# Low weight parts by adding DMA transfers, transposes on row halves, and a new pace of the convolution taps in a two-layer trunk

## The chip, the core and the metric

The kernel runs on one NeuronCore of a Trainium2 chip. The metric is the device time of one execution in microseconds (us). Engines are called as in the profile: PE (TensorE matmul) and PEld (its weight loads), DVE (VectorE), ACT (ScalarE), POOL (GpSimd) and SP (SyncE, which issues most DMAs). Each engine works its own instructions strictly in order and waits on semaphores for the others.

## What is computed

Two layers over 256 latent tokens and, in the first layer, 256 context tokens, model width 1024, all in float32. One layer is, shortened:

```
h = modulate(rmsnorm(x)); p = h @ w_in            # convolution, q/k/v and gate columns
u = a * sigmoid(g); u = dwconv1d(u, 31 taps); y_conv = silu(layernorm(u)) @ w_conv_out
y_attn = attention(q, k, v: windows + context keys) @ w_na_out      # 8 heads of 64
x = x + g1 * ((sigmoid(gc) * y_conv + sigmoid(ga) * y_attn) @ w_out)
x = x + g2 * conv_ffn(modulate(rmsnorm(x)))
```

The context stream goes through the same weights in the first layer only. The second layer has 256 latent tokens.

## The kernel before, in words

Activations lie with channels on partitions. To keep float32 accuracy at the speed of the rounded type fp32r, each weight and each activation is held as a high part (rounded) and a low part (the rest), and every product is three matmuls: high weight by high activation (L179), high weight by low activation (L180), low weight by high activation (L181). Weights come in units of 128 x 1024, eight 128 x 128 tiles. One unit in the first layer is 24 matmuls of 512 columns.

A unit is made ready by `wparts` and `wunit`: SP loads it into a `raw` buffer, ACT rounds it into `whi` (L160), DVE subtracts (`wlo = raw - whi`, L161). Each of the three names has 4 buffers, so a unit can be prepared while at most three others are still to be used, and ACT's copy waits until PE has finished the unit four back.

The order of the first layer around the change is: eight steps that make V and the first gated convolution input; then q and k of head pair 0 (two units), and for the pairs 1 to 3 two units of gated convolution input (`glu_groups`) and two of q and k; then five of the sixteen branch gates while attention ends; then the other gates, the convolution's layer norm, the branches and the output projection. A generator mechanism puts other work between: `group` calls `slot()` in the middle and at the end of a unit of 512 columns, and each `slot` advances all side jobs by one step. The side job `conv_run` issues `rate` convolution taps on DVE per slot (L591, 4 tiles of 31 taps). The gated inputs `us` are two buffers in the first layer (four in the second), so that `glu(2)` and `glu(3)` first issue every tap of the tile that had the buffer.

The side job `att` does attention in three stages, each a `step` later than the one before: `products` (q by k, matmuls with 64 rows, the two heads of a pair on the two row halves of the array, L440) followed by the softmax on DVE and ACT; `turn` (the softmax weights are transposed, PE into PSUM, ACT copies to `pT`, L494 and L499); `values` (V by the turned weights, L512). A step issues the turn of the last item, the values of the one before, and the products of the next, in that order. The first layer has six items (four latent pairs, two joint context items), the second four. The order in which instructions stand on each engine is fixed by a scheduler when the program is built.

Of the kernel before, what the change touches and what calls it, by code (L numbers as in the profile page):

```python
# [8 lines left out]
F32 = mybir.dt.float32  # L9
# [36 lines left out]
def trunk(ctx: ExitStack, tc: tile.TileContext, xt, cvec, crow, wall, wada, params, bias_t, rope_t, out):  # L46
# [136 lines left out]
    def group(ps, ws, xh, xl, c):  # L183
# [201 lines left out]
    class Attention:  # L385
# [3 lines left out]
        def __init__(self, l, eb, T, V, oh, ol):  # L389
            self.l, self.eb, self.T, self.V, self.oh, self.ol = l, eb, T, V, oh, ol  # L390
            self.todo, self.soft, self.pv, self.n, self.at = [], [], [], 0, 0
            self.ctx, self.pairs, self.last = [], 0, None

# [22 lines left out]
        def step(self, now=False):  # L416
            self.n += 1
            since = self.n - self.at
            if not now and (since < (4 if self.todo else 3 if self.soft else 2) or not self.todo and self.pairs < 4):
                return  # L420
            if self.todo and not now and self.n - self.todo[0][0] < 2:
                return
            self.at = self.n
# [7 lines left out]
            if self.todo:  # L431
                _, what, its = self.todo.pop(0)
                outs = [self.products(it, [psum(t) for t in tags]) for it, tags in zip(its, (("sc", "sc"), ("pt", "main")))]
                self.soft.append((what, its, [(self.scores if what == LAT else self.ctx_scores)(it, o) for it, o in zip(its, outs)]))

# [50 lines left out]
        def turn(self, what, its, pps):  # L486

            pts = [self.eb.tile([P, 4, S], F32, tag="pT", bufs=4, name=nm("pT")) for _ in range(2)]
            for n, tags in enumerate((("sc", "sc"), ("pt", "main"))):
                for i, pp in enumerate(pps[n]):  # L490
                    pt = psum(tags[i])
                    if what == LAT:
                        for kt in range(4):
                            pe.transpose(sl(pt, kt), sl(pp, kt), ident)  # L494
                        act.copy(pts[i][:, :, n * P : (n + 1) * P], pt.rearrange("p (k q) -> p k q", k=4))
                    else:
                        for t in range(2):
                            for kt in range(2):
                                pe.transpose(pt[:, kt * S + t * P : kt * S + (t + 1) * P], sl(pp, 2 * t + kt), ident)  # L499
                        act.copy(pts[i][:, 2 * n : 2 * n + 2, :], pt.rearrange("p (k q) -> p k q", k=2))  # L500
            js = [its[0][0]] if what == LAT else [it[0] for it in its]
            self.pv.append((what, js, pts))

        def values(self, what, js, pts, bank):
            po = psum(bank)
            kts = range(4) if what == LAT else range(2, 4)
            for n, j in enumerate(js):
                c = slice(n * S, (n + 1) * S)
                for kt in kts:
                    for i in range(2):  # L510
                        h = 2 * j + i
                        pe.matmul(  # L512
                            po[i * HD : (i + 1) * HD, c], self.V[kt][:, h * HD : (h + 1) * HD],
                            pts[i][:, 2 * n + kt - kts[0], :], start=kt == kts[0], stop=kt == kts[-1],
                        )
# [42 lines left out]
    for l in range(DEPTH):  # L558
# [5 lines left out]
        with ExitStack() if last else start as e1a:  # L564
# [27 lines left out]

            rate = [0]

            def conv_run():
                while True:
                    for _ in range(rate[0]):
                        if taps:
                            conv_tap(*taps.pop(0))
                    yield  # L600
# [32 lines left out]
            with ExitStack() as e1b:  # L633
# [111 lines left out]
                conv = conv_run()  # L745
                rate[0] = 3 if last else 2
                add_side(conv)
# [477 lines left out]
```

## Time and profile before

| | |
|---|---|
| median of 3 runs | 1127.63 us (1127.43 to 1128.85) |
| the profiled execution | 1127.64 us, its span 1125.9 us |
| granted clock of PE | 0.998 |
| PE busy | 1114.1 us, 99% of the span |
| DVE, ACT, POOL busy | 908.3, 563.6, 14.7 us |
| DMA read | 188.62 MB |

A row of the groups names line, engine, operation, output and inputs, shapes and count, then busy time, the mean of one in ns, and the idle time before them with what ended it. Matmuls overlap, so the distance between the starts of two says more about PE's pace than their durations. A row of the timeline is start and duration in us, engine, line, operation, count, and in square brackets the idle time before it with its releaser. A plain float32 matmul of the program stands as two in the trace; transposes and fp32r matmuls as one.

### The profile page before, as it was taken

The page shows a single profiled execution, that of the slowest core. Times are in us where ns is not written, and L with a number is a line of the kernel's source. Part 1 is how long each engine was busy: PE and PEld are TensorE (multiplying, and loading weights), DVE is VectorE, ACT ScalarE, POOL GpSimd, SP SyncE. Part 2 cuts the span into 40 slices and gives each one's busy share as a digit, 9 for nine tenths or more (in the row PEclk, how much of TensorE's full clock was granted, in tenths as well). Part 3 has the DMA queues.
Part 4 walks back from the last instruction along what each step waited for, and adds up shares of the span by engine and source line. Part 5 has one row for each costly group of instructions (what it writes and reads, how often), then busy time and mean ns, then how long its engine had stood idle before and what let it go on. Part 6 is the DMA issues. An engine that isn't in the chain of part 4 may idle for free.

```text
span 1125.9 us, 17731 instructions
## 1 busy us (share of the span) xinstructions
PE 1114.1 (99%) x6828; PEld 963.0 (86%) x6828; DVE 908.3 (81%) x1631; ACT 563.6 (50%) x934; POOL 14.7 (1%) x24
## 2 busy tenths in 40 slices
PE   9999999999999999999999999999999999999997
PEld 7778777787789988888888888989888999999997
DVE  5689999685778788888898555789996898988773
ACT  4347657542333543434343222544677667766642
POOL 0000000000000000000000000000000000000000
PEclk9999999999999999999999999999999999999999
DMA  9833231536734354554556665556433575565781
GB/s 364 282 94 103 75 118 38 206 97 214 245 118 138 114 161 150 168 169 149 168 171 215 219 191 186 180 181 187 145 126 121 167 250 163 188 194 181 219 268 58
DMA packets 53941, 190.83 MB, mean 169 GB/s; under 512 B 6240, under 2 KB 6496, under 8 KB 53856
## 3 DMA queue, kind: packets, MB, share of 16 engines
q1 hardware_dynamic: 53568, 189.65, 52.1%
q8 instruction: 54, 0.88, 0.3%
q14 instruction: 31, 0.25, 0.1%
q10 hardware_dynamic: 288, 0.04, 0.0%
HBM read 188.62 MB, written 1.05 MB: 168 GB/s over the span
## 4 chain that ended last, share of the span: by engine, by line
PE 83%; DVE 9%; issue 6%; ACT 2%; DMA 0%; POOL 0%; POOLq 0%; DVEq 0%; SPq 0%; ACTq 0%
PE main L179 24%; PE main L181 24%; PE main L180 24%; DVE cb L591 4%; PE main L644 4%; DVE wlo L161 1%; PE sc L181 1%; PE sc L179 1%; PE sc L180 1%; PE po L202 1%; PE po L512 1%; PE sc L129 1%; PE sc L440 0%; DMA sb<-in_crow 0%; PE sc L494 0%
## 5 line engine op out<-in xcount | busy, mean ns | idle before, releaser
L179 PE MATMUL main<-h,whi 128*128 128x256 f32 (+1 forms) x1328 | 446.7, 337 | 0.0
L181 PE MATMUL main<-h,wlo 128*128 128x256 f32 (+1 forms) x1328 | 442.9, 335 | 1.0 <-DVE wlo L161 1.0
L180 PE MATMUL main<-h,whi 128*128 128x256 f32 (+1 forms) x1328 | 442.2, 334 | 0.1
L160 ACT CAST whi<-raw 128x1024 fp32r<-128x1024 f32 (+1 forms) x244 | 252.3, 1039 | 285.5 <-PE main L180 131.5
L161 DVE TENSOR_TENSOR wlo<-raw,whi 128x1024 fp32r<-128x1024 f32 (+1 forms) x244 | 292.9, 1207 | 112.5 <-ACT whi L160 108.0
L179 PEld LDWEIGHTS main<-h,whi 128*128 128x128 f32 x1328 | 249.4, 188 | 32.1 <-issue 3.6
L181 PEld LDWEIGHTS main<-h,wlo 128*128 128x128 f32 x1328 | 249.3, 188 | 29.6 <-DVE wlo L161 1.5
L180 PEld LDWEIGHTS main<-h,whi 128*128 128x128 f32 x1328 | 249.8, 188 | 28.5 <-DVE h L367 0.5
L591 DVE SCALAR_TENSOR_TENSOR cb<-u,par,cb 128x512 f32<-128x512 f32 (+1 forms) x240 | 140.4, 609 | 1.4
L271 DVE CUSTOM_DVE_ANT_0 t<-raw,sb,par 128x1024 bf16<-128x1024 f32 x100 | 126.7, 1277 | 1.0 <-ACT sb L255 0.7
L179 PE MATMUL main<-fh,whi 128*128 128x256 f32 (+1 forms) x386 | 123.0, 319 | 0.0
L180 PE MATMUL main<-fl,whi 128*128 128x256 f32 (+1 forms) x386 | 122.9, 319 | 0.0
L181 PE MATMUL main<-fh,wlo 128*128 128x256 f32 (+1 forms) x386 | 122.9, 318 | 0.0
L180 PEld LDWEIGHTS main<-fl,whi 128*128 128x128 f32 x386 | 72.7, 188 | 5.6
L179 PEld LDWEIGHTS main<-fh,whi 128*128 128x128 f32 x386 | 72.7, 188 | 5.6
L181 PEld LDWEIGHTS main<-fh,wlo 128*128 128x128 f32 x386 | 72.7, 188 | 5.5
L963 ACT ACTIVATE t<-main,par 128x512 f32<-128x512 f32 (+1 forms) x82 | 50.6, 667 | 39.0 <-PE main L181 39.0
L964 DVE SCALAR_TENSOR_TENSOR t<-main,par,t 128x510 f32<-128x510 f32 (+1 forms) x82 | 47.5, 615 | 10.2 <-ACT t L963 9.8
L967 DVE SCALAR_TENSOR_TENSOR t<-main,par,t 128x510 f32<-128x510 f32 (+1 forms) x82 | 46.6, 609 | 0.0
L366 ACT ACTIVATE h<-t,mod 128x256 fp32r<-128x256 f32 x56 | 25.4, 502 | 36.1 <-DVE t L365 36.1
L898 DVE SCALAR_TENSOR_TENSOR x<-main,mod,x 128x256 f32<-128x256 f32 x48 | 22.1, 479 | 23.5 <-PE main L181 23.3
L644 PE MATMUL main<-whi,h 128*128 128x512 f32 x128 | 40.6, 402 | 0.1
(221 smaller groups left out, 1188.2 us busy)
## 6 DMA issues: line engine op xcount, KB each, us to landing
raw<-in_wall SPq DMA_DIRECT2D x239, 512.0 KB, 4.2
raw<-in_wada SPq DMA_DIRECT2D x88, 512.0 KB, 4.3
bias<-in_bias_t SPq DMA_DIRECT2D x8, 640.0 KB, 4.8
row<-in_wada SPq DMA_DIRECT2D x8, 512.0 KB, 4.7
sb<-in_crow SPq DMA_DIRECT2D x5, 512.0 KB, 6.0
x<-in_xt SPq DMA_DIRECT2D x8, 256.0 KB, 4.4
raw<-in_wall SPq DMA_DIRECT2D x8, 256.0 KB, 7.1
out<-t SPq DMA_DIRECT2D x3, 256.0 KB, 2.1
```

The source lines that it names most:

```text
L160: act.copy(hi[:, c], r[:, c])
L161: dve.tensor_tensor(lo[:, c], r[:, c], hi[:, c].bitcast(F32), ALU.subtract)
L179: pe.matmul(ps, w[0], xh, start=start, stop=False)
L180: pe.matmul(ps, w[0], xl, start=False, stop=False)
L181: pe.matmul(ps, w[1], xh, start=False, stop=stop)
L271: dve.tensor_tensor_reduce(tmp().bitcast(BF16), r, v, 1.0, pr(l, BADA + n, 1), ALU.mult, ALU.add, mods[l][:, n, s : s + 1])
L366: high = act.activation(hi[:, c], y[:, c], AF.Identity, bias=b)
L591: dve.scalar_tensor_tensor(cb[j], src, w, cb[j], ALU.mult, ALU.add)
L644: mm = pe.matmul(pv[t], h1[n == 1][k][:, c], w[n == 2][:, b], start=k + n == 0, stop=k == KD - 1 and n == 2)
L963: act.activation(c, pv_, AF.Identity, bias=pr(l, FDB + t, 1), scale=w[1])
L964: dve.scalar_tensor_tensor(c[:, :, 1:], pv_[:, :, : S - 1], w[0], c[:, :, 1:], ALU.mult, ALU.add)
L967: dve.scalar_tensor_tensor(c[:, :, : S - 1], pv_[:, :, 1:], w[2], c[:, :, : S - 1], ALU.mult, ALU.add)
```

## The change

It has four parts and two things that go with them.

1. For the 19 units of the first layer after V and the first gated input (`ADDED`: six of gated input, eight of q and k, five gates) the low part is no longer a DVE subtraction. ACT rounds the unit into `whi` as before, ACT writes `-whi` into `wlo`, and a DMA issued by POOL adds `raw` to it in place.
2. `turn` transposes halves of 64 rows: 32 transposes of 64 columns in the place of 16 of 128, alternating between the two row halves, which go to two PSUM banks. ACT's four copies pick the halves together into one tile `pT`.
3. The first layer has four buffers of gated input, so that no tile has to be finished early, and issues 2.25 taps per slot in place of 2.
4. In each layer the first turn stands alone: its step issues no products, and the next step issues only products.
5. The scratch for descriptors of POOL's DMAs is 1024 bytes in place of the default; the line numbers below L190 shift.

```diff
+ADDED = {(0, u) for u in range(U_IN, U_IN + 19)}
...
+    def wadded(l, u):
+        r = raw_unit(wall[l, u])
+        hi = wp.tile([P, UW], F32R, tag="whi", bufs=4, name=nm("whi"))
+        lo = wp.tile([P, UW], F32R, tag="wlo", bufs=4, name=nm("wlo"))
+        act.copy(hi, r)
+        act.mul(lo, hi.bitcast(F32), -1.0)
+        pool.dma_start(lo, r, accum_op=ALU.add)
+        return hi, lo
+
     def unit8(l, u, at=None):
-        w = wunit(l, u, at)
+        w = wadded(l, u) if (l, u) in ADDED else wunit(l, u, at)
...
+            alone = self.soft and not self.pv and not self.late
-            if not now and (since < (4 if self.todo else 3 if self.soft else 2) or not self.todo and self.pairs < 4):
+            if not now and since < (4 if self.todo or alone else 3 if self.soft else 2) and not self.late:
                 return
...
+            if self.late:
+                self.late, self.at = False, self.n
+                return self.issue()
+            if alone and not now:
+                self.late = True
...
-            pts = [self.eb.tile([P, 4, S], F32, tag="pT", bufs=4, name=nm("pT")) for _ in range(2)]
+            pT = self.eb.tile([P, 2, 4, S], F32, tag="pT", bufs=2, name=nm("pT"))
             for n, tags in enumerate((("sc", "sc"), ("pt", "main"))):
+                outs = [psum(t).rearrange("p (i s q) -> p i s q", i=2, s=4) for t in tags]
                 for i, pp in enumerate(pps[n]):
-                    pt = psum(tags[i])
+                    for s in range(4):
+                        src = s if what == LAT else s % 2 * 2 + s // 2
+                        for pt, r in zip(outs, HALF):
+                            pe.transpose(pt[:, i, s], sl(pp, src)[r], ident[r, r])
+                for pt, r in zip(outs, HALF):
                     if what == LAT:
-                        for kt in range(4):
-                            pe.transpose(sl(pt, kt), sl(pp, kt), ident)
-                        act.copy(pts[i][:, :, n * P : (n + 1) * P], pt.rearrange("p (k q) -> p k q", k=4))
+                        act.copy(pT[:, :, :, n * P + r.start : n * P + r.stop], pt)
...
-            NU_ = KC if last else 2
+            NU_ = KC
...
-                rate[0] = 3 if last else 2
+                rate[0] = 3 if last else 2.25
...
-    nc = bacc.Bacc("TRN2", target_bir_lowering=False, num_devices=1)
+    nc = bacc.Bacc("TRN2", target_bir_lowering=False, num_devices=1, dynamic_dma_scratch_size=1024)
```

The order of PE at the first turn of the first layer, before (`sc`, `pt` and `main` are PSUM banks, `pp` the softmax weights, `qk` the q and k of a pair, `h` the activations): the last matmul of the third unit after the first products, the turn, and at once the next products.

```order
L181 MATMUL main_972<-h_189,wlo_975 128x512
L494 MATMUL sc_1009<-ident,pp_845 128x128 x4
L494 MATMUL sc_1015<-ident,pp_853 128x128 x4
L494 MATMUL pt_1021<-ident,pp_861 128x128 x4
L494 MATMUL main_1027<-ident,pp_869 128x128 x4
L440 MATMUL sc_1033<-qk_967,qk_921 128x512
L440 MATMUL sc_1034<-qk_967,qk_921 128x512
```

The same place now, where the turn comes after two units and its halves alternate between two banks:

```order
L182 MATMUL main_937<-h_189,wlo_941 128x512
L517 MATMUL sc_975<-ident,pp_855 128x64
L517 MATMUL sc_976<-ident,pp_855 128x64
L517 MATMUL sc_975<-ident,pp_855 128x64
L517 MATMUL sc_976<-ident,pp_855 128x64
```

After the 32 halves follow the 24 matmuls of a whole unit, and only then the next products (L462 of the changed kernel). So the turn moved one unit ahead, and the products stayed where they were, behind the third unit. In the other nine turns the order of turn, values and products is as before.

ACT in the same place before, from the last rounding over the copies of the turned weights (`pT`) to the first two exponentials (`pp`) of the second softmax:

```order
L160 CAST whi_1320<-raw_1319 128x1024
L495 COPY pT_1007<-sc_1009 128x4x128
L495 COPY pT_1008<-sc_1015 128x4x128
L495 COPY pT_1007<-pt_1021 128x4x128
L495 COPY pT_1008<-main_1027 128x4x128
L461 ACTIVATE pp_1051,sm_1052<-sc_1033,mx_1049 128x512
L461 ACTIVATE pp_1059,sm_1060<-sc_1034,mx_1057 128x512
```

And now, where each rounding (L199) has a negation (L200) behind it:

```order
L520 COPY pT_974<-sc_975 128x8x64
L520 COPY pT_974<-sc_976 128x8x64
L520 COPY pT_974<-pt_995 128x8x64
L520 COPY pT_974<-main_996 128x8x64
L794 ACTIVATE qk_1021<-t_1015 128x256
L794 ACTIVATE qk_1021<-main_937 128x256
L199 CAST whi_1370<-raw_1368 128x1024
L200 ACTIVATE wlo_1371<-whi_1370 128x1024
L483 ACTIVATE pp_1080,sm_1081<-sc_1062,mx_1078 128x512
L483 ACTIVATE pp_1088,sm_1089<-sc_1063,mx_1086 128x512
```

The copies are out of the way of the second softmax, and a rounding and a negation of a unit stand ahead of it in their place. POOL had only sums and powers there; now its queue holds the 19 transfers in the order of the units, with the two sums of the convolution's layer norm (L868, L869) between them:

```order
+L201 DMA wlo_1596<-raw_1593 128x1024
+L868 TENSOR_TENSOR ss_2358<-cb_0_198,cb_1_199 128x512
+L201 DMA wlo_1644<-raw_1641 128x1024
+L201 DMA wlo_1784<-raw_1781 128x1024
+L201 DMA wlo_1823<-raw_1820 128x1024
+L201 DMA wlo_1981<-raw_1978 128x1024
+L869 TENSOR_TENSOR ss_2358<-ss_2358,cb_2_200 128x512
+L201 DMA wlo_2020<-raw_2017 128x1024
```

The sums moved ahead of the last five and of the last transfer, so these stand behind instructions that wait for DVE's taps.

More of the change, by code (lines that the diff above doesn't have):

```diff
@@ L391, in __init__ @@
             self.todo, self.soft, self.pv, self.n, self.at = [], [], [], 0, 0
-            self.ctx, self.pairs, self.last = [], 0, None
+            self.ctx, self.pairs, self.last, self.late = [], 0, None, False
         def pair(self, j, q, k, bt, last):
@@ L418, in step @@
             since = self.n - self.at
-            if not now and (since < (4 if self.todo else 3 if self.soft else 2) or not self.todo and self.pairs < 4):
+            alone = self.soft and not self.pv and not self.late
+            if not now and since < (4 if self.todo or alone else 3 if self.soft else 2) and not self.late:
                 return
-            if self.todo and not now and self.n - self.todo[0][0] < 2:
+            if not now and not alone and not self.todo and self.pairs < 4:
                 return
+            if not now and not alone and self.todo and self.n - self.todo[0][0] < 2:
+                return
+            if self.late:
[3 more added lines that the diff above has]
+                self.late = True
             self.at = self.n
@@ L430, in step, with issue @@
                 self.values(*work, "sc" if work[0] == CTX and not (soft or self.todo) else "po")
[L431 to L434, printed above, removed]
+            if self.todo and not self.late:
+                self.issue()
+        def issue(self):
+            _, what, its = self.todo.pop(0)
+            outs = [self.products(it, [psum(t) for t in tags]) for it, tags in zip(its, (("sc", "sc"), ("pt", "main")))]
+            self.soft.append((what, its, [(self.scores if what == LAT else self.ctx_scores)(it, o) for it, o in zip(its, outs)]))
         def product(self, out, q, k, c, d):
@@ L591, in conv_tap @@
                     dve.scalar_tensor_tensor(cb[j], src, w, cb[j], ALU.mult, ALU.add)
-            rate = [0]
+            rate = [0.0]
             def conv_run():
+                due = 0.0
                 while True:
-                    for _ in range(rate[0]):
+                    due += rate[0]
+                    while due >= 1:
+                        due -= 1
                         if taps:
```

12 lines of the change are left out of this document (5 added, 7 removed).

## The prediction

> **What bounds the kernel.** I read the page's first and fourth parts, then the windows of the stage that the change touches, then PE's own rows.
>
> ```profile
> span 1125.9 us, 17731 instructions
> PE 1114.1 (99%) x6828; PEld 963.0 (86%) x6828; DVE 908.3 (81%) x1631; ACT 563.6 (50%) x934; POOL 14.7 (1%) x24
> PE 83%; DVE 9%; issue 6%; ACT 2%; DMA 0%; POOL 0%; POOLq 0%; DVEq 0%; SPq 0%; ACTq 0%
> 58.00:200.00 142.00, 142.00 (x757) 112.03 (x756) 138.49 (x268) 93.48 (x186) 2.99 (x2) 1.00 0.28 85
> ```
>
> PE is busy 99% of the span and holds 83% of the chain that ended last. The last line is a window (stretch, its length, then PE, PEld, DVE, ACT and POOL, then clock, DMA share and GB/s) over the stage of the 19 units: from 58 to 200 us PE has no idle time, and DVE only 3.5 us of 142. The chain's 9% on DVE lies here. But PE does not wait for DVE: the starts of its matmuls of 512 columns follow each other every 0.23 us (and its pairs too: 83.04 and, two later, 83.50 below), 24 of a unit in 5.6. So DVE's relief is worth nothing by itself here. A gain must come from fewer PE microseconds, and a loss from a new wait of PE.
>
> **The turns on PE.** The six items of the first layer and the four of the second make ten. Eight are latent ones, with 8 transposes each to `sc` (64 in all):
>
> ```profile
> L494 PE MATMUL sc<-ident,pp 128*128 128x128 f32 x64 | 8.3, 273 | 0.0
> 100.68 1.04 PE L494 MATMUL sc<-ident,pp 128*128 128x128 f32 x8
> 101.55 0.60 PE L494 MATMUL pt<-ident,pp 128*128 128x128 f32 x4
> 101.99 0.60 PE L494 MATMUL main<-ident,pp 128*128 128x128 f32 x4
> 102.52 1.16 PE L440 MATMUL sc<-qk,qk 64*128 64x512 f32 x6
> 104.30 0.50 PE L179 MATMUL main<-h,whi 128*128 128x512 f32 x1
> 104.64 0.39 PE L180 MATMUL main<-h,whi 128*128 128x512 f32 x1
> ```
>
> Eight transposes take 101.55 - 100.68 = 0.87, so 0.109 each, 1.75 for 16; with the change to the next kind of matmul a turn is 102.52 - 100.68 = 1.84 us, ten are 18.4.
>
> No row has a transpose of 64 rows by 64 columns. The nearest rows are the products, whose two heads lie on the two row halves and go to two banks, as the new halves do:
>
> ```profile
> 81.90 0.40 PE L181 MATMUL main<-h,wlo 128*128 128x512 f32 x1
> 82.23 0.97 PE L440 MATMUL sc<-qk,qk 64*128 64x512 f32 x6
> 83.04 0.39 PE L440 MATMUL main<-qk,qk 64*128 64x512 f32 x1
> 83.04 0.39 PE L440 MATMUL pt<-qk,qk 64*128 64x512 f32 x1
> 83.50 0.39 PE L440 MATMUL main<-qk,qk 64*128 64x512 f32 x1
> 83.83 0.50 PE L179 MATMUL main<-h,whi 128*128 128x512 f32 x1
> 84.16 0.40 PE L180 MATMUL main<-h,whi 128*128 128x512 f32 x1
> 114.87 0.28 PE L440 MATMUL main<-qk,qk 64*128 64x256 f32 x1
> 114.99 0.28 PE L440 MATMUL main<-qk,qk 64*128 64x256 f32 x1
> ```
>
> Both members of a pair start together (83.04), a pair of 512 columns takes the 0.23 of one whole matmul, and a pair of 256 takes 0.12. So two half loads and two half matmuls run beside each other. Of a whole transpose with 128 columns in 0.109, a pair with 64 columns each would take 0.055 if the columns set it. The loads could set it instead:
>
> ```profile
> L494 PEld LDWEIGHTS sc<-ident,pp 128*128 128x128 f32 x64 | 7.4, 141 | 0.8
> L336 PEld LDWEIGHTS pt<-one,ss 128*128 128x128 f32 x32 | 4.2, 190 | 0.4 <-DVE ss L322 0.3
> L512 PEld LDWEIGHTS po<-pT,V 128*64 128x64 f32 x144 | 9.5, 136 | 5.4 <-issue 1.3
> 233.59 0.95 PE L336 MATMUL pt<-one,ss 128*128 128x1 f32 x8
> 234.40 0.47 PE L179 MATMUL main<-h,whi 128*128 128x512 f32 x1
> ```
>
> L336 moves one column per load, so its pace is that of a load of 128 columns: (234.40 - 233.59)/8 = 0.10. A load of 64 columns (L512) is recorded 54 ns shorter than L336's, and a transpose's load 49 ns shorter, like half a load: about 0.05. So I take 0.06 a pair, near the columns' 0.055 and the loads' 0.05, with 0.109 (no gain from pairing) as the upper end and 2 x 0.109 as the far one.
>
> The Trainium skill's "TensorE: Matmul & The Clock Gate", section "LDWEIGHTS (loading the stationary operand)", speaks against this: a load's time goes with its columns and not with its rows, at columns/1.2 ns, so a half of 64 rows by 128 columns would load as long as a whole, 0.107 us, and by it 16 pairs take at least 1.71 us, an estimate that gives no gain. The trace agrees with it for L336 (0.10), and the 141 ns of a transpose's load against 190 speak against it here.
>
> Entering the row halves costs 82.23 - 81.90 - 0.23 = 0.10; a whole transpose needed none. Leaving costs 102.52 - 101.99 - 4 x 0.109 = 0.09 towards another tiled kind; towards whole matmuls 0.10 and 0.10 more in the first of them (83.83 to 84.16 is 0.33). A new turn is 16 x 0.06 + 0.10 + 0.09 = 1.15, 0.69 less than 1.84, at eight places 5.5. At the two lone turns: before, turn and products with their exit are 104.64 - 0.23 - 100.68 = 3.73, now 0.96 + 0.30 for the turn and 84.16 - 0.23 - 82.13 = 1.80 for products alone, 3.06, so 0.67 less each, 1.3. Together 6.9 us if nothing else ends later.
>
> **ACT behind the turns.** The negations are 19 more instructions on ACT. Their price is bounded by a rounding of the same size, 1.05, and by that times 720/615 (scaled against rounded at 512 columns), 1.23; I take 1.07, 20 us in all.
>
> ```profile
> L160 ACT CAST whi<-raw 128x1024 fp32r<-128x1024 f32 x238 | 248.8, 1050 | 285.5 <-PE main L180 131.5 <-DMA raw<-in_wall 128.7 <-issue 11.8
> L464 ACT ACTIVATE pp<-pp,ri 128x512 f32<-128x512 f32 x32 | 22.1, 720 | 1.7 <-DVE ri L463 1.7
> L160 ACT CAST whi<-raw 128x512 fp32r<-128x512 f32 x6 | 3.6, 615 | 0.0
> 104.70 0.69 ACT L461 ACTIVATE pp<-sc,mx 128x512 f32<-128x512 f32 x1 [1.05 <-DVE mx L458]
> 109.25 0.71 ACT L464 ACTIVATE pp<-pp,ri 128x512 f32<-128x512 f32 x1
> 111.82 1.95 PE L512 MATMUL po<-pT,V 128*64 128x256 f32 x16
> 112.81 1.07 ACT L495 COPY pT<-sc 128x512 f32<-128x512 f32 x2
> 132.37 1.05 ACT L160 CAST whi<-raw 128x1024 fp32r<-128x1024 f32 x1 [1.51 <-PE main L180]
> 113.70 1.21 PE L440 MATMUL sc<-qk,qk 64*128 64x256 f32 x12
> ```
>
> 93.5 + 20 of 142 us leaves ACT room, but not at each turn. A rounding waits for the unit that ends just as a turn starts (132.37), and now the negation follows it ahead of the copies that free the banks of the next products. Turn and values (113.70 - 111.82 = 1.88) cover 1.15 + 1.88 = 3.03 us from the turn's start. At the first layer's second turn the softmax ended with no slack (109.25 + 0.71 = 109.96; the turn, 1.84 ahead of the values at 111.82, began at 109.98) and the copies of `sc` end at 113.9, 3.9 after the turn's start: they, not PE, set the next products, so the 0.69 is lost. And its softmax now stands behind a rounding and a negation that start when its products do: 2.1 us, then 5.3 us of softmax (104.70 to 109.96 before), against 1.5 of products and 5.6 of a unit: 0.4 late. At the third turn rounding, negation and four copies of 0.5 take 4.1 against 3.03 + 0.8 of products to `sc` (83.04 - 82.23): 0.25 late. The other turns have a copy slack of 0.5 us or more. Sum: 6.9 - 0.7 - 0.4 - 0.25 = 5.6.
>
> **The transfers.** What was a subtraction on DVE is now a negation and a transfer, and PE needs it at the third matmul of the unit. The tightest is the third of the 19, the first that is rounded when PE is already at work on the first:
>
> ```profile
> L161 DVE TENSOR_TENSOR wlo<-raw,whi 128x1024 fp32r<-128x1024 f32 x238 | 288.8, 1220 | 112.2 <-ACT whi L160 108.0 <-PE sc L181 3.2 <-PE sc L440 0.3
> 58.18 1.05 ACT L160 CAST whi<-raw 128x1024 fp32r<-128x1024 f32 x1
> 59.14 0.58 ACT L777 COPY V<-main 128x512 f32<-128x512 f32 x1
> 59.81 0.39 PE L179 MATMUL main<-h,whi 128*128 128x512 f32 x1
> raw<-in_wall SPq DMA_DIRECT2D x239, 512.0 KB, 4.2
> raw<-in_wall SPq DMA_DIRECT2D x8, 256.0 KB, 7.1
> ```
>
> Rounded at 59.2, negated at 60.8; needed at 59.81 + 2 x 5.6 + 2 x 0.23 = 71.4: 10.6 us of room, more later (three units, 16.7, less 2.2). A plain transfer of this size lands in 4.2, and in halves behind others in 7.1. No row shows an adding one, which reads twice and writes once: between 4.2 and three plain legs, 12.6, nearest to 7.1 since other loads run beside it. I take it as hidden; at 12.6 it would cost 2.0. `raw` is held longer by as much, against a turn-round of its four buffers of 4 x 5.6 = 22 us. On POOL the sums L868 and L869 wait for taps of tiles 1 and 2, which DVE's order ends at the rotations of the third and fourth k, before the transfers behind them are ready: no cost. The two further fills of `us` run at the start before POOL is wanted. The other taps and DVE's 19 x 1.2 = 23 us of relief move work that PE does not wait for: nothing, either way.
>
> The profiled execution took 1127.64, the median 1127.63, so the forecast is 1127.64 - 5.6 = 1122.0.
>
> **Rivals.** A, pairs give nothing: 0.109 a pair, a turn 1.75 + 0.19 = 1.94, so 8 x 0.10, 2 x 0.1 at the lone ones and 0.4 of the late softmax: 1129.0. For it speaks the pace of L336, against it the pairs of the products.
> B, the adding transfer is late (the slower side). Place: the third unit's first matmul with `wlo`. From 10.6 us on each us more stops PE as long; it turns the gain over, by 0.2%, from 10.6 + 5.6 + 2.3 = 18.5; at 20 us the time is 1122.0 + 9.4 = 1131.4. Later units have a turn-round of (5.6 + 2.1 + 20)/4 = 6.9 against 142/19 = 7.5 of PE, so the loss is paid mostly once. For it: POOL prepares the transfer itself, and DVE leaves it 3.5 of 142 us without a DVE instruction; against it: less than half of the 10.6 us suffices for a plain one. The Trainium skill's "SBUF — State Buffer", section "SBUF: two separate sides", has this as a rule: descriptors of a GpSimd transfer are held up while VectorE runs certain instructions, with 620 ns becoming 3100; no run here shows it.
> C, halves run one after the other, each as long as a whole: 32 x 0.109 = 3.5, +1.84 a turn: 1146.
> D, ACT takes back the gain at every turn of the first layer: 2.8 of 5.6 us left out and 1 us lost: 1126.
>
> **Chances.** Forecast 0.60 (its own range 1119.5 to 1125.3, from 0.05 a pair without new waits, to 0.08 a pair), A 0.14, B 0.12, C 0.06, D 0.08, of which a quarter stays under 1125.4. Changes under 0.2% (2.3 us) are about what a measurement of this kernel cannot tell from none. Faster: 0.62; within 0.2%: A and the rest of D, 0.20; slower: B and C, 0.18. The range from 1119.5 to 1131 leaves out C, most of B and a little below.
>
> **What would show it.** The 16 pairs of a turn should start every 0.06 us and a turn reach the values in 1.15; the start of the matmuls with `wlo` in the 19 units should show no idle time released by a DMA; the transfers should land in 4 to 10 us. PE's idle time released by ACT should rise by about 1 us near 110 to 140 us. I am wrong if the pairs start every 0.11 or more, or if PE waits for `wlo` at 71 us.

## The result, and the profile after

The changed kernel takes 1135.29 us (median of 4, 1133.97 to 1137.62) against 1128.24 for the kernel before: a ratio of 1.0065, with a 95% interval of 1.0045 to 1.0085. It is 7 us slower, where 6 us less were forecast. The profiled execution has a span of 1134.3 us, 8.4 more than before.

From the page after: span, busy times, the chain's shares and the row of the new transfers.

```profile
span 1134.3 us, 18108 instructions
PE 1115.6 (98%) x6988; PEld 958.9 (85%) x6988; DVE 892.2 (79%) x1612; ACT 581.7 (51%) x954; POOL 32.0 (3%) x45
PE 77%; DVE 16%; ACT 4%; issue 2%; DMA 1%; SPq 0%; DVEq 0%; ACTq 0%
wlo<-raw POOLq DMA_DIRECT2D x19, 512.0 KB, 6.2
```

DVE lost 16 us of work, yet its share of the chain rose from 9% to 16%, and PE's fell from 83% to 77%. The transfers land in 6.2 us, and no matmul of the 19 units waits for one. The first lone turn shows that the cheap turn came as forecast:

```profile
95.51 0.71 PE L517 MATMUL sc<-ident,pp 64*128 64x64 f32 x16
96.06 0.22 PE L517 MATMUL pt<-ident,pp 64*128 64x64 f32 x1
...
96.12 0.22 PE L517 MATMUL pt<-ident,pp 64*128 64x64 f32 x1
...
96.65 0.50 PE L180 MATMUL main<-h,whi 128*128 128x512 f32 x1
```

A pair every 0.06 us (96.06, 96.12), and 96.65 - 95.51 = 1.14 for the turn. So what PE was to save, it saves. Three places give more than that back. The first is the last turn of the first layer, here on PE:

```profile
190.74 0.79 PE L517 MATMUL sc<-ident,pp 64*128 64x64 f32 x16
193.35 0.27 PE L517 MATMUL pt<-ident,pp 64*128 64x64 f32 x1 [1.82 <-ACT pp L504]
...
194.87 2.81 PE L535 MATMUL po<-pT,V 128*64 128x256 f32 x16
197.61 0.80 PE L180 MATMUL main<-h,whi 128*128 128x512 f32 x1
198.21 0.63 PE L181 MATMUL main<-h,whi 128*128 128x512 f32 x1
198.63 0.63 PE L182 MATMUL main<-h,wlo 128*128 128x512 f32 x1
```

The turn takes 194.87 - 190.74 = 4.13 instead of 1.14, because the second half of the softmax weights is not ready. ACT scales it in four parts, first the kernel before, then the changed one:

```profile
189.30 1.72 ACT L482 ACTIVATE pp<-pp,ri 128x256 f32<-128x256 f32 x4
```

```profile
192.77 1.72 ACT L504 ACTIVATE pp<-pp,ri 128x256 f32<-128x256 f32 x4
```

This is 3.47 us later, and PE takes each part as it comes, about every 0.4 us from 193.35 on; so the turn loses more than the 1.82 us of the first wait. After it the values take 2.74 (1.88 before), and matmuls start 0.42 to 0.60 apart instead of 0.23. The windows (stretch, length, PE, PEld, DVE, ACT, POOL, then granted clock) say why:

```profile
190.00:195.00 5.00, 2.94 (x38) 1.92 (x38) 3.30 (x7) 4.98 (x17) 0.00 (x0) 1.00 0.00 0
195.00:200.00 5.00, 5.00 (x23) 3.17 (x24) 0.00 (x0) 4.99 (x9) 0.00 (x0) 0.66 0.00 0
```

The granted clock falls, to 0.66 in the mean from 195 to 200 us, and from the start of these values to that of the last ones (201.33) 1.6 us more are lost. The reason for the late softmax stands on DVE. Before, up to the first maxima of the last context item:

```profile
174.62 6.04 DVE L591 SCALAR_TENSOR_TENSOR cb<-u,par,cb 128x512 f32<-128x512 f32 x9
180.59 1.21 DVE L161 TENSOR_TENSOR wlo<-raw,whi 128x1024 fp32r<-128x1024 f32 x1
181.73 0.73 DVE L591 SCALAR_TENSOR_TENSOR cb<-u,par,cb 128x512 f32<-128x512 f32 x1
182.39 0.41 DVE L519 TENSOR_TENSOR ol<-po,oh 128x256 fp32r<-128x256 f32 x1
182.72 0.73 DVE L591 SCALAR_TENSOR_TENSOR cb<-u,par,cb 128x512 f32<-128x512 f32 x1
183.39 1.27 DVE L472 TENSOR_REDUCE mx<-sc 128x2 f32<-128x512 f32 x2
```

And after:

```profile
162.87 6.25 DVE L614 SCALAR_TENSOR_TENSOR cb<-u,par,cb 128x512 f32<-128x512 f32 x8
...
182.47 1.22 DVE L162 TENSOR_TENSOR wlo<-raw,whi 128x1024 fp32r<-128x1024 f32 x1
183.61 2.32 DVE L614 SCALAR_TENSOR_TENSOR cb<-u,par,cb 128x512 f32<-128x512 f32 x3
185.85 0.42 DVE L542 TENSOR_TENSOR ol<-po,oh 128x256 fp32r<-128x256 f32 x1
186.18 0.74 DVE L614 SCALAR_TENSOR_TENSOR cb<-u,par,cb 128x512 f32<-128x512 f32 x1
186.84 1.28 DVE L494 TENSOR_REDUCE mx<-sc 128x2 f32<-128x512 f32 x2
...
193.25 0.16 DVE L501 RECIPROCAL ri<-sm 128x2 f32<-128x2 f32 x1
201.38 1.23 DVE L162 TENSOR_TENSOR wlo<-raw,whi 128x1024 fp32r<-128x1024 f32 x1 [7.97 <-ACT whi L161]
```

The scalar_tensor_tensor rows are taps. The scheduler filled the places of the removed subtractions with taps. A long row of them is nothing new (nine at 174.62 before, eight at 162.87 now); what differs is how many stand ahead of the last maxima: from 58 us on, 101 taps and 19 subtractions before, 120 taps and 2 subtractions now. The maxima of the fourth pair, behind the eight taps, already start 3.5 us late (169.37 for 165.83), but its turn had that much to spare. DVE runs its queue in order, so the last maxima start 3.45 us later than before, although the products on PE end within 0.2 us of where they did, and this is the 3.47 us by which ACT is late. Right behind the softmax DVE then has nothing to do for 8 us; its last tap starts at 191.78, and at 206.03 before. The groups of the stretch from 60 to 200 us show the same for the whole stage, first before, then after: 114 taps, and 120, each a little longer.

```profile
L591 DVE SCALAR_TENSOR_TENSOR cb<-u,par,cb 128x512 f32<-128x512 f32 x114 | 81.8, 739 | 0.6
```

```profile
L614 DVE SCALAR_TENSOR_TENSOR cb<-u,par,cb 128x512 f32<-128x512 f32 x120 | 90.7, 761 | 2.0
```

The second place is the layer norm of the convolution. PE and DVE there, from the timeline:

```profile
258.49 0.69 DVE L888 TENSOR_TENSOR sl<-cb,sh 128x512 fp32r<-128x512 f32 x1 [0.31 <-ACT sh L887]
259.10 2.35 DVE L162 TENSOR_TENSOR wlo<-raw,whi 128x1024 fp32r<-128x1024 f32 x2
260.37 0.57 PE L182 MATMUL main<-h,wlo 128*128 128x512 f32 x1 [2.13 <-DVE wlo L162]
```

And a window behind it:

```profile
262.00:264.00 2.00, 2.00 (x6) 1.58 (x5) 2.00 (x5) 0.81 (x1) 0.00 (x0) 0.50 0.92 258
```

The low part of a gate (still a subtraction) stands on DVE behind the whole layer norm, PE waits 2.1 us for it, and from 262 to 264 the clock is at 0.50. The third place is the second layer, in small waits.

The table gives, for every kernel of this study, how much later than in the kernel before five landmarks of PE start in its profiled execution: the first products (82.23 us before), the last values of the first layer's attention (197.19), the second round of modulation products behind the branches' gates (266.38), the first products of the second layer (796.88), the sum of its layer norm (879.82), and then the span. The first column is scatter of the first microseconds, before the changed stage.

| kernel | 82 | 197 | 266 | 797 | 880 | span |
|---|---|---|---|---|---|---|
| changed kernel | +0.3 | +4.1 | +7.4 | +7.4 | +9.1 | +8.4 |
| half | +0.3 | +0.7 | +1.3 | +1.4 | +1.3 | +0.7 |
| added19 | +0.9 | +3.3 | +2.9 | +3.0 | +3.0 | +1.9 |
| taps | +0.4 | +0.6 | +5.4 | +5.4 | +5.5 | +4.7 |
| alone | +0.3 | +0.2 | +0.7 | +0.8 | +2.0 | +4.9 |
| few_taps | +0.7 | +0.7 | -0.1 | 0.0 | 0.0 | -0.7 |
| few_taps_half | -0.1 | -2.5 | -3.1 | -3.0 | -4.4 | -5.4 |
| rate275 | +0.7 | +3.6 | +5.7 | +5.8 | +7.8 | +7.3 |
| half_added_held | -0.3 | -1.2 | +1.4 | +1.5 | +1.4 | +0.5 |
| added30 | -0.2 | +4.4 | +11.5 | +11.8 | +13.6 | +13.0 |
| hctx30 | +0.3 | -2.0 | +9.3 | +9.3 | +11.0 | +10.3 |
| no_alone | +0.8 | +4.5 | +6.2 | +6.9 | +7.1 | +6.3 |
| b30h2 | 0.0 | -0.2 | +9.0 | +9.0 | +9.0 | +9.8 |
| r24 | -0.1 | +3.6 | +2.8 | +2.9 | +4.6 | +3.7 |
| q16 | +0.2 | -0.6 | -1.4 | -1.3 | +0.5 | -0.4 |
| p16 | +0.3 | -0.5 | -1.3 | -1.2 | -0.9 | -1.9 |
| z16 | -0.3 | -1.1 | -1.8 | -1.8 | -1.9 | -2.9 |

### The profile page after: what moved, and what is told of

Read it like the earlier page. It is cut to its first block, busy times and chain, and to the rows that moved or that the text cites. A ratio compares the mean times of both kernels' runs of the same rounds, so it can differ in the third digit from the quotient of the medians.

```text
span 1134.3 us, 18108 instructions
## 1 busy us (share of the span) xinstructions
PE 1115.6 (98%) x6988; PEld 958.9 (85%) x6988; DVE 892.2 (79%) x1612; ACT 581.7 (51%) x954; POOL 32.0 (3%) x45
## 4 chain that ended last, share of the span: by engine, by line
PE 77%; DVE 16%; ACT 4%; issue 2%; DMA 1%; SPq 0%; DVEq 0%; ACTq 0%
PE main L180 22%; PE main L182 22%; PE main L181 22%; DVE cb L614 7%; PE main L670 4%; DVE wlo L162 3%; ACT pp L483 1%; PE sc L180 1%; PE sc L182 1%; PE sc L181 1%; PE po L213 1%; DVE qk L795 1%; ACT pp L486 1%; ACT whi L161 1%; PE po L535 1%
## 5 line engine op out<-in xcount | busy, mean ns | idle before, releaser
L161 ACT CAST whi<-raw 128x1024 fp32r<-128x1024 f32 (+1 forms) x225 | 232.3, 1037 | 276.4 <-DMA raw<-in_wall 146.3
L162 DVE TENSOR_TENSOR wlo<-raw,whi 128x1024 fp32r<-128x1024 f32 (+1 forms) x225 | 270.0, 1207 | 119.9 <-ACT whi L161 118.8
L614 DVE SCALAR_TENSOR_TENSOR cb<-u,par,cb 128x512 f32<-128x512 f32 (+1 forms) x240 | 144.6, 620 | 2.6
```

Of the source, the lines that this page charges most:

```text
L161: act.copy(hi[:, c], r[:, c])
L162: dve.tensor_tensor(lo[:, c], r[:, c], hi[:, c].bitcast(F32), ALU.subtract)
L614: dve.scalar_tensor_tensor(cb[j], src, w, cb[j], ALU.mult, ALU.add)
```

## The experiments: each part alone

Theory "queue": the freed places on DVE fill up with taps, so that softmax and low parts come later. Rivals: the new pace of the taps does it ("pace"), or the negations make ACT late ("ACT"). Four kernels each take one part of the change, on the kernel before. The smaller scratch is in these four and in all the kernels that follow; it was not tried by itself.

**half**: the new `turn` and `values` only.

> The kernel before with the turns on row halves alone. All theories: a pair of halves every 0.06 us, a turn about 1.15 us to the values instead of 1.84, ten turns. If PE keeps what it saves, 1128.2 - 6.9 = 1121.3; if ACT's copies and DVE's softmax hold the next products at two or three turns, as in the changed kernel, 1123 to 1125. If the new waits in the second layer (near 838, 875 and 901 to 912 us) come with the halves, its 4 turns gain nothing and the time is about 1125.

1128.71 us, ratio 1.0006 (0.9997 to 1.0015). No gain at all, which none of the numbers had foreseen. In the first layer the third to fifth turns keep their 0.7 us (from the turn's start to the last product 4.30, 4.29 and 4.44, for 4.99, 4.99 and 5.13 before). The first keeps 0.1, the second loses 0.5, where the products wait for ACT's copies. The last turn loses more than all of it:

```profile
189.64 0.71 PE L506 MATMUL sc<-ident,pp 64*128 64x64 f32 x16
191.48 0.27 PE L506 MATMUL pt<-ident,pp 64*128 64x64 f32 x1 [1.12 <-ACT pp L493]
...
193.00 0.87 PE L524 MATMUL po<-pT,V 128*64 128x256 f32 x6
```

193.00 - 189.64 = 3.36 for this turn, 1.5 more than a whole one cost before. Here too the maxima start later on DVE than in the kernel before (184.96 for 183.39), behind a row of eight taps, although no subtraction was removed.

**added19**: `wadded` and `ADDED` only.

> The kernel before with the 19 adding transfers alone. Theory queue (DVE's freed places are filled with taps that run ahead of the softmax, so that the last context softmax ends about 2 us after its turn is due, PE stands still and its clock falls behind it): slower by 3 to 5, 1131 to 1133, with a wait of PE for ACT pp inside the last turn of the first layer. Theory pace (the 2.25 taps and four buffers do it): within 1 us of 1128.2, no such wait. Theory ACT (the negations make ACT late): slower by 1.5 to 2.5, by waits of PE for ACT pT after the second and third turn.

1129.65 us, ratio 1.0016 (1.0007 to 1.0026). The wait in the last turn is there (1.62 us, by the softmax weights L493), and landmark 197 is 2.4 later than the one at 82. Its size is below the forecast of "queue", for no slow clock follows here, and 0.4 us come back behind the attention; 1.7 us is the amount of "ACT". But the place speaks for "queue", and between 58 and 200 us this is the only wait that the profile shows for PE: none by ACT's copies.

**taps**: `NU_ = KC` and 2.25 taps a slot only.

> The kernel before with four buffers of gated input and 2.25 taps a slot alone. Theory pace: slower by 4 to 5, 1132 to 1133, with PE waiting inside the last turn of the first layer. Theory queue: no wait in the turns, but the layer norm's sum stands half a unit later on PE (120 matmuls of units behind the last values instead of 108), and the wait for wlo at the start of the branches near 252 us is longer: slower by 0 to 2.5, 1128 to 1130.5.

1132.04 us, ratio 1.0034 (1.0023 to 1.0046). The amount is that of "pace", the place that of "queue": nothing in the turns, everything between 197 and 266, with this row of PE and this window (clock 0.50) in it.

```profile
258.38 0.50 PE L182 MATMUL main<-h,wlo 128*128 128x512 f32 x1 [2.13 <-DVE wlo L162]
```

```profile
260.00:262.00 2.00, 2.00 (x7) 1.52 (x6) 2.00 (x5) 0.85 (x1) 0.00 (x0) 0.50 0.89 283
```

With two buffers the taps of a tile were forced out early by the next two gated inputs. With four, the list empties only at the pace, and the layer norm (whose side job first drains the list) starts one slot, half a unit, later: 120 matmuls of units behind the last values instead of 108.

**alone**: the new `step` only.

> The kernel before with only the first turn of each layer standing alone. Each lone turn and each lone set of products pays the way in and out of the row halves once more (2 x 0.1 to 0.2 us), so 1128.2 + 0.4 = 1128.6 if nothing else moves. If the new waits of the second layer come with the lone turn, that moves a unit there, slower by 2 to 4: 1130 to 1132.

1129.91 us, ratio 1.0016 (1.0007 to 1.0026), 1128.64 to 1132.62. 1.2 us are lost between 797 and 880; the profiled execution lies at the upper end and has one more wait of 1.84 us for a low part at 931 us. This lies between the two numbers, just under the second.

The four parts lose 0.8 + 1.7 + 4.1 + 2.0 = 8.6 us, somewhat more than the whole loses (7.1).

## The experiments: where the saving of the halves goes

**few_taps** and **few_taps_half**: the kernel before, and `half`, without the branch that issues the taps 1 to 30 of each tile, in both layers, so the convolution is left out of their result.

```diff
                 if t == 0:
                     dve.tensor_scalar(cb[j], src, w, pr(l, DWB + j, 1), ALU.mult, ALU.add)
-                else:
-                    dve.scalar_tensor_tensor(cb[j], src, w, cb[j], ALU.mult, ALU.add)
```

> The kernel before without 30 of the 31 taps of each tile (only the first of each, so the convolution is left out of the result; some 81 us less work of DVE in the first layer). Theory queue (DVE's order is full, and softmax stands in it behind taps): PE did not wait for it before, so within 2 us of 1127.9; 1126 to 1128. It is the base for the next kernel.

> The same with the turns on row halves. Theory queue: with DVE free the softmax is ready when PE comes to a turn earlier, so the halves keep what they save, 5 to 6.5 us under the kernel without taps: 1120 to 1122. Theory ACT (ACT's copies of the turned weights and its roundings set the next products): half of it or less is kept, -1 to -3.

1126.44 us (ratio 0.9988, 0.9979 to 0.9997) and 1123.11 (0.9956, 0.9942 to 0.9971): the halves bring 3.3 us here, and nothing with the taps. That lies between the two theories. The last turn of the first layer is now without a wait:

```profile
188.70 0.71 PE L506 MATMUL sc<-ident,pp 64*128 64x64 f32 x16
...
189.84 1.95 PE L524 MATMUL po<-pT,V 128*64 128x256 f32 x16
```

So with the taps on DVE the halves are worth 4.1 us less (0.8 lost, for 3.3 gained), of the 6.9 that PE was to save. Of the rest, some 1.4 us stay lost in the second layer and 1 at the first turns of the first layer, where ACT sets the next products. In the changed kernel the second turn looks so (timeline, ACT and then PE):

```profile
110.37 1.03 ACT L199 CAST whi<-raw 128x1024 fp32r<-128x1024 f32 x1
111.42 1.28 ACT L632 ACT_TABLE_LOAD   x1
112.71 0.60 ACT L632 ACTIVATE t<-main 128x512 f32<-128x512 f32 x1
113.21 1.07 ACT L520 COPY pT<-sc 128x512 f32<-128x512 f32 x2
113.84 1.34 PE L462 MATMUL sc<-qk,qk 64*128 64x256 f32 x11 [0.93 <-ACT pT L520]
```

A rounding, the load of a function table and a sigmoid stand ahead of the copies that free the banks. They stood there in the kernel before too (the copies of `sc` at 112.81); a shorter turn only comes to the same wait earlier.

**half_added_held**: `half` with the 19 transfers, and each tap behind the maxima of the last softmax that the program has issued before it.

```diff
+            def conv_tap(j, t):
+                with tc.issue_after(att.maxed.ins) if l == 0 and att.maxed else ExitStack():
+                    conv_tap_(j, t)
```

(`att.maxed` is the reduction of `scores` or `ctx_scores` last issued.)

> The kernel before with halves and the 19 transfers, and each tap of the first layer that follows the products of an item in the program also behind its softmax maxima in DVE's order. Layer norm at 121 matmuls. Theory queue: the wait in the last turn (2 to 2.4 us in the kernels with transfers) is gone and the halves keep 3 to 4 us in the first layer, against 1 to 2.5 for the later layer norm: 1125 to 1128. If DVE's order is not the cause, the sum of the parts, 1127.9 + 0.8 + 1.7 = 1130.4, or more.

1129.32 us, ratio 1.0011 (1.0001 to 1.002), between the two. At 197 it is 1.2 us ahead of the kernel before, where `half` is 0.7 behind and `added19` 3.3. So the order on DVE is a cause of the loss in the attention. But the taps now end late, and 2.6 us are lost up to 266, in waits for the layer norm's sum, for its `rs` and for a low part.

## The experiments: the layer norm's place

**rate275**: the changed kernel with another number.

```diff
-                rate[0] = 3 if last else 2.25
+                rate[0] = 3 if last else 2.75
```

> The changed kernel with 2.75 taps a slot for 2.25. DVE's order around the last softmax stays as in the changed kernel, only the layer norm of the convolution stands two units earlier on PE (72 matmuls behind the last values in place of 120; 108 in the kernel before). Theory place (the late layer norm makes the first low part of the branches late, 2.3 us at 258 us, and 0.7 to 1.2 at its own sum): 2.5 to 4.5 less than the 1135.3 of the changed kernel, 1131 to 1133. Theory queue alone: no change, 1135.

1135.28 us, ratio 1.0068 (1.0051 to 1.0085). No change, so "place" as I had put it is wrong. The layer norm did come earlier, but there is again a wait for a low part:

```profile
249.58 0.50 PE L182 MATMUL main<-h,wlo 128*128 128x512 f32 x1 [1.67 <-DVE wlo L162]
```

**added30**: the changed kernel with transfers for the 11 other gates too, so that no subtraction is left in that stage. **hctx30**: the same with taps held behind the maxima of context items, and 2.4 taps a slot.

```diff
-ADDED = {(0, u) for u in range(U_IN, U_IN + 19)}
+ADDED = {(0, u) for u in range(U_IN, U_IN + 30)}
```

> The changed kernel with adding transfers for the 11 remaining gates of the first layer too (30 units). Theory queue, at the layer norm: PE waits 2.3 us at 258 because the subtraction of a gate stands on DVE behind the layer norm's work; without subtractions in that stage the wait goes, 2 to 3 less than 1135.3: 1132.3 to 1133.3. The wait in the last turn stays at about 2 us, since DVE's order ahead of it is still full of taps. If the wait comes from the layer norm itself, it only moves to the first matmul with sh or sl: 1135.

> The same with every tap that follows the products of a context item in the program held behind that item's maxima on DVE, and 2.4 taps a slot (the layer norm then stands at 108 matmuls, as in the kernel before). Theory queue, at the softmax: the wait in the last turn (2.1 us) and the slow clock behind it (1.6 us) go, 3 to 4 less than with 30 units alone: 1129 to 1130. If the held taps make the layer norm's sum late instead, that gives back 1 to 2: 1130 to 1132. If DVE's order is not the cause, no change, 1133.

1140.98 us (ratio 1.0123, 1.0108 to 1.0138) and 1137.53 (1.0083, 1.0068 to 1.0099). Both are far from what I expected. The wait for `wlo` is gone in both, but there is a larger one for POOL. Here the timeline of `hctx30`, POOL, ACT and PE:

```profile
241.37 1.05 ACT L199 CAST whi<-raw 128x1024 fp32r<-128x1024 f32 x1 [8.45 <-DMA raw<-in_wall]
...
243.90 0.87 POOL L201 DMA_DIRECT2D wlo<-raw  x1 [12.27 <-ACT wlo L200]
244.47 1.37 POOL L357 TENSOR_TENSOR rs<-red,mhalf 128x4 f32<-128x4 f32 x1
245.89 1.11 PE L362 MATMUL po<-ident,rs 128*128 128x128 f32 x4 [3.60 <-POOL rs L357]
```

POOL also works in order. A transfer stands ahead of the layer norm's power and waits 12 us for ACT's negation, and ACT waits 8 of them for the load of that unit. The held taps did what was expected: `hctx30` ends the attention 2.0 us ahead of the kernel before, `added30` 4.4 behind.

**b30h2**: `half_added_held` with the 30 units.

> The kernel before with halves, 30 adding transfers, and all taps of the first layer that follow an item's products held behind its maxima; no lone turns, two buffers, two taps a slot; layer norm at 108 matmuls. Theory queue: the attention of the first layer keeps 1 to 2 us as with 19 transfers and held taps, and the 3.3 us that this lost at the layer norm become 0 to 1.5, since no subtraction stands behind it: 1126 to 1128, between 2 us less than the kernel before and the same. If the layer norm's wait is of another cause, 1129.3 as with 19.

1136.33 us, ratio 1.0079 (1.0064 to 1.0094), again far above what was expected: level at 197, and 9 us lost at the layer norm, with the same wait (4.4 us for `rs`) as the largest part. **no_alone**: the changed kernel with the `step` of before.

> The changed kernel without the lone turns. If the parts add, 2.0 less: 1133.3. If the lone turns gave their share back by freeing ACT for the second softmax, 1135 to 1136.

1134.89 us, ratio 1.0064 (1.0047 to 1.0081), 0.4 less than the changed kernel, with a scatter (1132.69 to 1136.16) that holds both theories; it does not decide. In the profiled execution the second layer's loss (797 to 880) is 0.2 in place of 1.7.

**r24**: the changed kernel with 2.4 taps a slot, which moves the layer norm's sum by half a unit only, to 108 matmuls.

> The changed kernel with 2.4 taps a slot for 2.25. DVE's order at the attention is the same; the layer norm's sum stands at 108 matmuls behind the last values, as in the kernel before, instead of 120, half a unit earlier. Theory phase (the low part of a gate stands on DVE behind the layer norm's work, which ends some 26 us after its sum; whether PE waits depends on where in a unit of 5.6 us that falls, so an even number of half units leaves none and an odd one 2.3): the wait at 258 goes, 2.3 less, 1133.0; the last turn's wait stays. Theory size (the wait comes with a fuller DVE): the wait stays, 1135.

1132.3 us, ratio 1.0038 (1.0025 to 1.0051), 3.0 less than the changed kernel. The wait is gone, the last turn's is not (1.81 us). That is what theory "phase" said: the wait depends on where in a unit of 5.6 us DVE comes out of the layer norm: at 108 matmuls none, half a unit later (120) 2.1, and one and a half units earlier than 108 (72) 1.7. Moving it from 120 to 72 is two whole units, and so left the wait in place.

## The experiments: the taps put right

**q16**: `r24` with the last 15 taps of the last tile held behind the maxima of the last context item, and nothing else changed.

```diff
+                with tc.issue_after(att.maxed.ins) if l == 0 and j == 3 and t >= 16 and att.maxed else ExitStack():
+                    conv_tap_(j, t)
```

> The same with the taps from the seventeenth of the last tile on held behind the maxima of the last context item on DVE. Theory queue: the last turn finds its softmax ready, 2.1 us of wait and 1.6 of slow clock go and the turn keeps its 0.7: 3.5 to 5 less than with 2.4 taps alone, 1128 to 1129.5. If ACT or POOL holds the last turn as well, 1 to 2 less.

1127.67 us, ratio 0.9999 (0.999 to 1.0008), 4.6 less than `r24`, as "queue" had it. DVE has done 109 taps, and no longer 120, when the last maxima start. **p16** has the same hold, halves and transfers on the kernel before; **z16** is `q16` with the lone turn in the first layer alone (`alone = self.l == 0 and ...`).

> The kernel before with halves, the 19 transfers and the same held taps (two buffers, two taps a slot, no lone turns, layer norm at 108 matmuls). The first layer ends its attention 0.5 to 1 us ahead of the kernel before and its layer norm pays nothing (as with the 19 transfers alone, -0.4); the second layer gives nothing: 1126.5 to 1128, so between 1.4 us less than before and the same.

> As q16, the lone turn in the first layer only. The lone turn of the second layer cost 1.2 us in the profiles of the changed kernel and of the kernel with lone turns alone: 1 to 2 less than q16, 1126 to 1128. If the parts only trade places, as q16.

p16 takes 1125.76 us (ratio 0.9983, 0.9973 to 0.9993), z16 1125.51 (0.9982, 0.9972 to 0.9991), each a little less than expected. Both beat both kernels: by 2.1 and 2.4 us the one before, and by some 10 the changed one. In `z16`, DVE and PE at the last softmax and turn:

```profile
181.52 1.28 DVE L495 TENSOR_REDUCE mx<-sc 128x2 f32<-128x512 f32 x2
...
190.13 0.71 PE L518 MATMUL sc<-ident,pp 64*128 64x64 f32 x16
...
191.28 1.95 PE L536 MATMUL po<-pT,V 128*64 128x256 f32 x16
```

The maxima start at 181.52, and no longer at 186.84; the turn takes 1.15, and no slow clock follows. From `z16` to the changed kernel there are three small edits (the held taps, 2.4 for 2.25, no lone turn in the second layer), so these three things hold the 10 us.

## Why the prediction was wrong

- **PE's saving (right in size, wrong in effect).** "0.06 a pair" measured 0.06, the 1.15 of a turn 1.14. By the Trainium skill's "TensorE: Matmul & The Clock Gate", section "LDWEIGHTS (loading the stationary operand)", a half would load as long as a whole (0.107 us); the estimate of at least 1.71 us for 16 pairs that the prediction drew from it did not come true, for 16 pairs start within 0.99 us (95.51 to 96.50), and the measurement decides. But "6.9 us if nothing else ends later" did not hold: with the halves alone nothing is left of it.
- **"The other taps and DVE's 19 x 1.2 = 23 us of relief move work that PE does not wait for: nothing, either way."** This is the step that failed. I had read "from 58 to 200 us PE has no idle time" as "PE does not wait for DVE". It only meant that each softmax came in time, at some turns only just: at the last one ACT ended the last part at 191.02, and PE came to it at 191.80. (The third and fifth turns had 4 us or more.) DVE was full (138.5 of 142 us), and the page's 9% of DVE in the chain, which I named and put aside, was the sign. The order itself shows the taps: I quoted POOL, ACT and PE, and did not look at what stood on DVE where the subtractions had been. In the place of "nothing" stand, in the changed kernel's profile, 3.0 us for the last turn (4.13 for 1.14) and 1.6 of slow clock. That DVE's order is the cause is shown by `q16`: with 15 taps held behind these maxima, and nothing else changed, the wait goes and 4.6 us come back.
- **Four buffers of gated input, which the prediction gave no cost.** Taps no longer forced out empty their list later, and so the layer norm starts half a unit later: 4.1 us when alone. In its profile 2.1 are the wait for `wlo` and 0.8 a longer wait for ACT's `t` at 210 (1.33 for 0.58); most of the rest goes with the slow clock.
- **ACT behind the turns (right at one place, too small in all).** The second turn: the forecast let the copies of `sc` end 3.9 us behind its start; the products start at 113.84 - 109.82 = 4.02. The second softmax, for which I had 0.4, was not late: no wait stands ahead of the turn at 109.82. The third turn, where I had 0.25 of loss, kept its whole 0.70. But the fourth and fifth, where I had a slack of 0.5 us or more, kept nothing: from the turn's start to the last product they take 5.07 and 5.21, for 4.99 and 5.13 before, because ACT comes to the copies of `sc` only at 162.69 and 179.44, behind roundings and copies of other work. So the first five turns of the first layer together kept less than 0.1 us (0.32 late at the first products, 0.26 at the start of the last turn), where the forecast had 2.1.
- **The lone turns.** "0.67 less each" is lost again: alone they cost 2.0 us, 1.2 of them in the second layer; why the waits there come is located but not explained.
- **The second layer.** Four turns were to give 2.8. With the halves alone 0.1 is kept from 797 to 880 (+1.4 and +1.3), without the taps 1.4 (-3.0 and -4.4). So the taps take a part there too.
- **The transfers (right).** 6.2 us against 7.1 taken, with no wait; rival B did not come. The Trainium skill's "SBUF — State Buffer", section "SBUF: two separate sides", has descriptors of GpSimd's transfers held up while VectorE runs certain instructions; nothing of this is seen here between issue and landing, with DVE busy 128 of 140 us from 60 to 200; whether DVE's instructions in this stage are of the kind that the page means, no run settles. What did hold up a queue was POOL's order, at 30 units.
- **The rivals.** D (ACT takes back the gain at every turn of the first layer, 1126) came near to what the first five turns did, but still forecast a gain. A, B and C were slower, by causes that did not come: the pairs start every 0.06 us, and no transfer was waited for. None had DVE's order or the place of the layer norm.

## What to carry to other kernels

In this kernel an engine that is full and works in order had no spare place: work removed from it was replaced by what the scheduler found, and that stood in front of the one instruction that was due. Before crediting a saving on the bounding engine, look at each hand-over (here softmax to turn, low part to matmul) for its slack, and if it is near zero, free the queue that feeds it first. The halves were worth nothing with the taps in the way and 3 us without them, and the full change moved from +7 to -2.4 us by three small edits, of which the hold on 15 taps was worth 4.6.

## What the runs showed of the hardware

- PE's clock can fall after short waits. Behind waits of 1.82 us (last turn, changed kernel), 1.84 (`alone`, at 931) and 2.13 (at 260, changed kernel, and at 258, `taps`) the granted clock is 0.50 for some 3 us, behind 1.12 (`half`), 1.62 (`added19`) and 1.67 (`rate275`) it stays at 1.00. But the length of the wait alone does not decide: in `no_alone` the same wait of 2.13 us (at 261) is followed by a clock of 1.00, in `b30h2` one of 1.89 (at 237) too, and in `hctx30` the clock fell to 0.50 behind 1.11 (at 236). For example `added19`, over its wait and behind it:

```profile
190.00:195.00 5.00, 3.38 (x20) 2.40 (x19) 3.97 (x9) 5.00 (x18) 0.00 (x0) 1.00 0.00 0
195.00:200.00 5.00, 5.00 (x31) 3.38 (x32) 0.00 (x0) 4.97 (x10) 0.00 (x0) 1.00 0.00 0
```

  Where the clock fell, a wait of 2 us cost almost 4: from 197 to 266 the changed kernel loses 3.2 us, and `no_alone`, with the same wait and no slow clock, 1.7. Executions of one kernel differ in this: the four of the changed kernel had mean granted clocks of 0.997, 0.997, 0.994 (the profiled one) and 0.992, at 1133.97, 1134.48, 1136.10 and 1137.62 us. The Trainium skill's "TensorE: Matmul & The Clock Gate", section "HAM oscillation — how this bites in real kernels", warns of idle gaps above about 3.4 us; these were shorter. What decides, and whether the transposes around the wait count as idle, no run here settles.
- A transfer that adds 512 KB into a buffer on the chip landed in 5.3 to 6.3 us (median) in all kernels that had it, against 4.2 for a plain load in the kernel before.
- Taps of the same shape follow each other every 0.66 us in some rows and every 0.79 in others, in both kernels: nine in 6.04 us at 174.62 and ten in 7.84 at 189.88 in the kernel before, eight in 6.25 at 162.87 in the changed one. Why, no run here shows.
